# Start addresses of TensorE's operands in SBUF moved to multiples of 512 bytes

## The chip, the core and the metric

The kernel runs on one core of a Trainium2 chip. The metric is the device time of one execution in microseconds (us). A profile of one execution gives the start and the length of every instruction on TensorE (PE, and PEld for its weight loads), VectorE (DVE), ScalarE (ACT), GpSimd (POOL) and the queues that start transfers (SP and others).

## What is computed

One layer of a decoder trunk for 256 tokens of width 2048, in float32. Each of four branches (block attention, gated convolution, indexed sparse attention, attention into 256 memory tokens) reads columns of one wide projection of the normalized input:

```
xn = rms_norm(x, ln_g)
(a_q, a_k, a_v, a_g, c_b, c_c, c_h, c_g, s_q, s_k, s_v, s_g, m_q, m_g,
 i_q, i_k, i_w, r_a, r_c, r_s, r_m) = [xn @ w for w in cols]
...
y_c = c_b * short_conv(c_c * c_h, conv_w, conv_b) * jax.nn.silu(c_g)
...
merged = (sigmoid(r_a) * (y_a @ w_branch[0]) + sigmoid(r_c) * (y_c @ w_branch[1])
          + sigmoid(r_s) * (y_s @ w_branch[2]) + sigmoid(r_m) * (y_m @ w_branch[3]))
return x + merged @ w_out
```

A last RMSNorm follows. Nearly all work is matrix products of 256 rows with weights that are read once, 266 MB in all.

## The kernel before

Each float32 product is made of three products in float32r, a form that TensorE multiplies in one pass. `split` (L103) writes an operand as `hi`, the rounded value (a CAST on ScalarE, L104), and `lo`, the rest (a subtraction on VectorE, L105); then hi·hi, hi·lo and lo·hi are summed in PSUM. `split_weights` (L114) loads 1 MB of weights with a transfer on SP's queue into one of four `raw` buffers and splits it into pairs of `hi` and `lo`, four buffers each. The activations are split once and kept: `x_hl` (the normalized input), `m16a` and `m16b` (the memory tokens, `m_hl` in the code), `y` (a branch's gated result), `mt` (the merged result, in the place of `x_hl`), `x_sums`; in the attentions `part` and `pt`.

Two forms of product fill TensorE:

- `products_t` (L135, lines L138 to L140): the weights `hi` or `lo` are the stationary operand (128 columns), the activations the moving one (256 columns). The tile written is `acc` (or `first`). `project_t` makes all the sections that are wanted transposed.
- `products` (L157, lines L159 to L161): 128 columns of activations are stationary, 512 columns of `hi` or `lo` move. The tiles written are `w` (branch projections, activations `y`), `r` and `v` (gate and memory projections, activations `x_hl` or `m16a`/`m16b`), `o` (the last projection, activations `mt`; its last two blocks have 256 columns), and `m`, `z`, `r`, `x`, `y` in `by_halves` (L222), a form of the gate projections with fewer products and more additions. In the trace a product is written out<-moving,stationary.

Transposes (`pp`) take `ident` as the moving operand and float32 tiles (`pr`, `merged`) as the stationary one.

Tiles come from pools (L54 to L60). A pool's tiles lie one after another in each partition, from multiples of 32 bytes on, and the pools follow each other: `const`, `big`, `rawp`, `spl` (`hi`, `lo`), `prt` (`part`), `ptp` (`pt`), `tmp`. So the sum of the small constants sets where all large tiles begin, and the convolution's `u` ([128, 8, T + 2] float32, 8,256 bytes, in one place with `kt`) sets where everything behind it begins. All large tiles and all slices that TensorE reads are multiples of 512 bytes long, so within the large pools the remainder of the start by 512 is the same for all tiles of a group. In the built program before the change:

| tiles | first byte in the partition | remainder by 512 |
|---|---|---|
| `ident` | 16,768 | 384 |
| `x_col` / `m_col` | 18,944 / 20,000 | 0 / 32 |
| `x_hl`, `mt` | 24,352 | 288 |
| `qt`, `m16b`, `m16a`, `kt`, `x_sums`, `merged` | 57,120 and on | 288 |
| `vv`, `y` | 106,336 and on | 352 |
| `raw`, `hi`, `lo`, `part`, `pt` | 139,104 and on | 352 |
| `pr` | 220,064 | 416 |

The order of the instructions on each engine is set by a scheduler when the program is built. On POOL the first instructions are four loads of constants (`g_x`, `g_m`, `cw`, `cb`, L77 to L80), then `ident` and the masks. `g_x` is first read by `split_tokens` (L130).

## Time and profile before

| | |
|---|---|
| median of 3 runs | 1,399.23 us (1,397.75 to 1,400.73) |
| profiled execution | 1,398.06 us, its span 1,396.3 us |
| TensorE busy | 1,380.4 us (99%), 8,796 products |
| VectorE busy | 933.4 us (67%) |
| ScalarE busy | 729.2 us (52%) |
| POOL busy | 11.0 us (1%) |
| granted TensorE clock, mean | 0.997 |
| transfers | 269.5 MB, mean 193 GB/s |

TensorE's busy time is made of overlapping products whose ends are modelled: a product of 256 columns is listed with 276 to 281 ns, while the next one starts 113 to 118 ns after it. The pace is therefore read from starts, either in the timeline (first column: start in us) or as a window's length over the number of products in it.

### The profile page before, as it was taken

The page shows a single profiled execution, that of the slowest core. Times are in us where ns is not written, and L with a number is a line of the kernel's source. Part 1 is how long each engine was busy: PE and PEld are TensorE (multiplying, and loading weights), DVE is VectorE, ACT ScalarE, POOL GpSimd, SP SyncE. Part 2 cuts the span into 40 slices and gives each one's busy share as a digit, 9 for nine tenths or more (in the row PEclk, how much of TensorE's full clock was granted, in tenths as well). Part 3 has the DMA queues.
Part 4 walks back from the last instruction along what each step waited for, and adds up shares of the span by engine and source line. Part 5 has one row for each costly group of instructions (what it writes and reads, how often), then busy time and mean ns, then how long its engine had stood idle before and what let it go on. Part 6 is the DMA issues. An engine that isn't in the chain of part 4 may idle for free.

```text
span 1396.3 us, 21263 instructions
## 1 busy us (share of the span) xinstructions
PE 1380.4 (99%) x8796; PEld 1243.9 (89%) x8796; DVE 933.4 (67%) x1123; ACT 729.2 (52%) x991; POOL 11.0 (1%) x25
## 2 busy tenths in 40 slices
PE   9999999999999999999999999999999999999997
PEld 9998998789998898878999899878999998878887
DVE  7687764774848884596546885487547558787654
ACT  7663675453445684354445585445343345545443
POOL 1000000000000000000000000000000000000000
PEclk9999999999999999999999999999999999999999
DMA  9774545375554735537553746537555654736551
GB/s 343 291 271 173 191 156 180 128 266 189 172 197 133 254 128 183 189 135 247 188 193 133 243 150 211 182 125 266 183 181 187 225 192 148 265 130 241 183 197 73
DMA packets 49969, 269.49 MB, mean 193 GB/s; under 512 B 6656, under 2 KB 17456, under 8 KB 19024
## 3 DMA queue, kind: packets, MB, share of 16 engines
q1 hardware_dynamic: 48960, 264.03, 55.0%
q0 software_dynamic: 624, 3.31, 0.6%
q8 instruction: 69, 1.13, 0.3%
q10 hardware_dynamic: 288, 0.79, 0.1%
q14 instruction: 28, 0.23, 0.0%
HBM read 265.88 MB, written 2.10 MB: 192 GB/s over the span
## 4 chain that ended last, share of the span: by engine, by line
PE 85%; DVE 8%; DMA 3%; issue 2%; ACT 2%; SPq 0%; POOLq 0%; POOL 0%; DVEq 0%; ACTq 0%
PE acc L138 13%; PE acc L140 13%; PE acc L139 13%; DVE lo L105 5%; PE w L160 4%; PE w L161 4%; PE w L159 4%; PE r L159 4%; PE r L161 4%; PE r L160 4%; PE o L160 2%; PE o L161 2%; PE o L159 2%; DMA raw<-in_w_n 1%; PE y L160 1%
## 5 line engine op out<-in xcount | busy, mean ns | idle before, releaser
L105 DVE TENSOR_TENSOR lo<-raw,hi 128x1024 fp32r<-128x1024 f32 (+1 forms) x538 | 640.0, 1202 | 416.5 <-ACT hi L104 414.4
L104 ACT CAST hi<-raw 128x1024 fp32r<-128x1024 f32 (+1 forms) x538 | 552.2, 1032 | 547.8 <-PE acc L139 196.4
L139 PE MATMUL acc<-x_hl,hi 128*128 128x256 f32 x1520 | 426.0, 280 | 0.0
L138 PE MATMUL acc<-x_hl,hi 128*128 128x256 f32 x1520 | 425.4, 280 | 0.5 <-ACT qt L155 0.5
L140 PE MATMUL acc<-x_hl,lo 128*128 128x256 f32 x1520 | 425.8, 280 | 0.0
L140 PEld LDWEIGHTS acc<-x_hl,lo 128*128 128x128 f32 x1520 | 288.1, 190 | 0.1
L138 PEld LDWEIGHTS acc<-x_hl,hi 128*128 128x128 f32 x1520 | 284.8, 187 | 0.9 <-ACT qt L155 0.7
L139 PEld LDWEIGHTS acc<-x_hl,hi 128*128 128x128 f32 x1520 | 284.8, 187 | 0.2
L159 PE MATMUL w<-hi,y 128*128 128x512 f32 x256 | 99.9, 390 | 0.0
L161 PE MATMUL w<-hi,y 128*128 128x512 f32 x256 | 99.7, 389 | 0.0
L160 PE MATMUL w<-lo,y 128*128 128x512 f32 x256 | 99.6, 389 | 0.0
L159 PE MATMUL r<-hi,x_hl 128*128 128x512 f32 x248 | 98.3, 396 | 0.0
L161 PE MATMUL r<-hi,x_hl 128*128 128x512 f32 x248 | 97.9, 395 | 0.0
L160 PE MATMUL r<-lo,x_hl 128*128 128x512 f32 x248 | 97.6, 394 | 0.0
L159 PEld LDWEIGHTS w<-hi,y 128*128 128x128 f32 x256 | 48.1, 188 | 10.0
L161 PEld LDWEIGHTS w<-hi,y 128*128 128x128 f32 x256 | 48.1, 188 | 10.0
L160 PEld LDWEIGHTS w<-lo,y 128*128 128x128 f32 x256 | 48.1, 188 | 9.9
L161 PEld LDWEIGHTS r<-hi,x_hl 128*128 128x128 f32 x248 | 46.7, 188 | 10.6
L160 PEld LDWEIGHTS r<-lo,x_hl 128*128 128x128 f32 x248 | 46.7, 188 | 10.4
L159 PEld LDWEIGHTS r<-hi,x_hl 128*128 128x128 f32 x248 | 46.9, 189 | 10.2
L161 PE MATMUL o<-hi,mt 128*128 128x512 f32 (+1 forms) x160 | 55.3, 347 | 0.0
L160 PE MATMUL o<-lo,mt 128*128 128x512 f32 (+1 forms) x160 | 55.1, 346 | 0.0
(246 smaller groups left out, 1860.7 us busy)
## 6 DMA issues: line engine op xcount, KB each, us to landing
raw<-in_w_t SPq DMA_DIRECT2D x92, 1024.0 KB, 5.0
raw<-in_w_n SPq DMA_DIRECT2D x80, 1024.0 KB, 4.9
raw<-in_w_branch SPq DMA_DIRECT2D x32, 1024.0 KB, 5.3
raw<-in_w_out SPq DMA_DIRECT2D x16, 1024.0 KB, 4.8
raw<-in_w_mem_k SPq DMA_DIRECT2D x8, 1024.0 KB, 6.4
raw<-in_w_mem_v SPq DMA_DIRECT2D x8, 1024.0 KB, 5.5
raw<-in_w_t SPq DMA_DIRECT2D x16, 256.0 KB, 5.9
raw<-in_memT SPq DMA_DIRECT2D x2, 1024.0 KB, 8.8
```

Source lines behind the costliest of these rows:

```text
L104: nc.scalar.copy(out=hi, in_=src)
L105: nc.vector.tensor_sub(out=lo, in0=src, in1=hi.bitcast(F32))
L138: nc.tensor.matmul(o, lhsT=hi, rhs=a[:, 0], start=(k == 0), stop=False)
L139: nc.tensor.matmul(o, lhsT=hi, rhs=a[:, 1], start=False, stop=False)
L140: nc.tensor.matmul(o, lhsT=lo, rhs=a[:, 0], start=False, stop=(k == nk - 1))
L159: nc.tensor.matmul(o, lhsT=ah, rhs=hi, start=start, stop=False)
L160: nc.tensor.matmul(o, lhsT=ah, rhs=lo, start=False, stop=False)
L161: nc.tensor.matmul(o, lhsT=al, rhs=hi, start=False, stop=stop)
```

## The change

A tile `fill` of 56 float32 values (224 bytes) is added to the constants' pool and set to zero on POOL. The convolution's `u` gets a place of 8 · (T + 16) float32 values (8,704 bytes), of which it uses the first 8 · (T + 2) with the same row step as before.

```
     cb = const.tile([P, 8], F32, name="cb")
+
+    fill = const.tile([P, 56], F32, name="fill")
+    nc.gpsimd.memset(fill, 0.0)
     nc.gpsimd.dma_start(out=g_x, in_=ln_g)
...
     cc = to_heads("qt", C_C)
-    u = big.tile([P, 8, T + 2], F32, name="u", tag="kt")
+    u = big.tile([P, 8 * (T + 16)], F32, name="u", tag="kt")[:, :8 * (T + 2)].rearrange("p (c t) -> p c t", c=8)
     nc.gpsimd.memset(u[:, :, 0:2], 0.0)
```

With it the built program places the tiles so (the last byte used is 228,928, before 228,256):

| tiles | first byte in the partition | remainder by 512 |
|---|---|---|
| `ident` | 16,992 | 96 |
| `x_col` / `m_col` | 19,168 / 20,224 | 224 / 256 |
| `x_hl`, `mt` | 24,576 | 0 |
| `qt`, `m16b`, `m16a`, `kt`, `x_sums`, `merged` | 57,344 and on | 0 |
| `vv`, `y` | 107,008 and on | 0 |
| `raw`, `hi`, `lo`, `part`, `pt` | 139,776 and on | 0 |
| `pr` | 220,736 | 64 |

On TensorE, VectorE, ScalarE and SP the instructions stand in the same order as before, in the same shapes. On POOL one is added. At the start of the program POOL has, before the change (loads of `g_x`, `g_m`, `cw`, `cb`, then the first setups):

```order
6 L77 DMA g_x<-in_ln_g 128x16
7 L78 DMA g_m<-in_mem_ln_g 128x16
8 L79 DMA cw<-in_conv_w 128x24
9 L80 DMA cb<-in_conv_b 128x8
10 masks.py:197 MEMSET ident 128x128
```

And at the same place with the change:

```order
6 L79 MEMSET fill 128x56
7 L80 DMA g_x<-in_ln_g 128x16
8 L81 DMA g_m<-in_mem_ln_g 128x16
9 L82 DMA cw<-in_conv_w 128x24
10 L83 DMA cb<-in_conv_b 128x8
11 masks.py:197 MEMSET ident 128x128
```

The MEMSET of `fill` stands ahead of the four loads, and all that follows on POOL is one place later; line numbers behind it are three higher.

## Rows read from the trace of the kernel before

**Rows 1.** The page: engines' busy time; granted clock by fortieth; the chain by engine.
```profile
PE 1380.4 (99%) x8796; PEld 1243.9 (89%) x8796; DVE 933.4 (67%) x1123; ACT 729.2 (52%) x991; POOL 11.0 (1%) x25
...
PEclk9999999999999999999999999999999999999999
...
PE 85%; DVE 8%; DMA 3%; issue 2%; ACT 2%; SPq 0%; POOLq 0%; POOL 0%; DVEq 0%; ACTq 0%
```

**Rows 2.** Timeline of PE from 380 us: start us, length us, engine, line, operation.
```profile
380.07 0.28 PE L140 MATMUL acc<-x_hl,lo 128*128 128x256 f32 x1
...
384.94 0.28 PE L138 MATMUL acc<-x_hl,hi 128*128 128x256 f32 x1
```

**Rows 3.** Timeline of PE from 700 us.
```profile
700.12 0.28 PE L139 MATMUL acc<-x_hl,hi 128*128 128x256 f32 x1
...
704.95 0.28 PE L138 MATMUL acc<-x_hl,hi 128*128 128x256 f32 x1
```

**Rows 4.** Timeline of PE from 578 us.
```profile
578.07 0.39 PE L159 MATMUL w<-hi,y 128*128 128x512 f32 x1
...
582.83 0.39 PE L159 MATMUL w<-hi,y 128*128 128x512 f32 x1
```

**Rows 5.** Windows: by_halves, `r`, `o`; length, busy us by engine (count), clock, DMA share.
```profile
265.00:303.00 38.00, 37.15 (x161) 29.64 (x160) 32.93 (x31) 21.17 (x23) 0.00 (x0) 1.00 0.65 224
...
858.00:897.00 39.00, 39.00 (x169) 31.59 (x168) 17.77 (x15) 17.34 (x18) 0.00 (x0) 1.00 0.56 189
...
1307.00:1364.00 57.00, 57.00 (x251) 46.77 (x250) 31.45 (x31) 24.47 (x30) 0.00 (x0) 1.00 0.55 187
```

**Rows 6.** Transposes of `merged`: timeline of PE, and the line's lengths (min/median/max ns).
```profile
1227.41 1.04 PE L633 MATMUL pp<-ident,merged 128*128 128x128 f32 x8
...
L633 PE MATMUL pp<-ident,merged x32: 272/272/273, 1227.4 to 1306.9; 128*128 128x128 f32 x32
```

**Rows 7.** The start: timeline of POOL and ACT, and the landing of `g_x`.
```profile
1.24 0.70 POOL L77 DMA_DIRECT2D g_x<-in_ln_g  x1 [0.79 <-POOLq L706]
...
3.66 0.12 POOL L93 MEMSET mhalf<- 128x2 f32 x1
...
4.46 0.90 ACT L130 ACTIVATE x_hl<-xraw,g_x 128x256 fp32r<-128x256 f32 x2
...
DMA to landing us min/median/max: 2.9/2.9/2.9
```

**Rows 8.** Groups of weight loads by shape: count, busy us, mean ns.
```profile
L139 PEld LDWEIGHTS acc<-x_hl,hi 128*128 128x128 f32 x1504 | 282.6, 188 | 0.2
...
L633 PEld LDWEIGHTS pp<-ident,merged 128*128 128x128 f32 x32 | 3.7, 141 | 0.5
...
L285 PEld LDWEIGHTS pr<-ident,x_col 128*128 128x128 f32 x2 | 0.2, 134 | 0.0
```

**Rows 9.** Groups of products by shape: count, busy us, mean ns, idle before.
```profile
L139 PE MATMUL acc<-x_hl,hi 128*128 128x256 f32 x1504 | 421.5, 280 | 0.0
...
L159 PE MATMUL w<-hi,y 128*128 128x512 f32 x256 | 99.9, 390 | 0.0
...
L160 PE MATMUL m<-lo,x_sums 128*128 128x512 f32 x84 | 34.1, 406 | 3.3 <-DVE lo L105 3.3
```

**Rows 10.** Windows, instructions of tile `acc` alone: length, PE busy us (count), PEld.
```profile
357.00:433.00 76.00, 76.00 (x671) 75.85 (x670) 0.00 (x0) 5.49 (x15) 1.00 0.53 181
...
665.00:756.00 91.00, 90.62 (x768) 90.60 (x768) 0.00 (x0) 5.72 (x15) 1.00 0.53 182
...
986.00:1168.00 182.00, 180.95 (x1536) 181.05 (x1536) 6.22 (x16) 5.60 (x15) 1.00 0.56 190
```

**Rows 11.** Timeline of PE from 156.3 us, in the memory attention.
```profile
156.39 0.28 PE L140 MATMUL acc<-x_hl,lo 128*128 128x256 f32 x1
156.50 0.28 PE L354 MATMUL yp<-pt,part 128*128 128x256 f32 x1
...
157.69 0.28 PE L355 MATMUL yp<-pt,part 128*128 128x256 f32 x1
```

## The prediction

> **What bounds the kernel now.** [...] Busy TensorE says nothing of its pace, because matmuls overlap, so the timeline comes next: the distance from one start to the next.

> [...] From 380.07 to 384.94 us there are 43 steps of 256 columns, 113.3 ns each [rows 2]. From 700.12 to 704.95 us there are 41 steps of the same form on the same tiles, 117.8 ns each [rows 3]. From 578.07 to 582.83 us there are 21 steps of 512 columns, 226.7 ns each [rows 4]. The window from 858 us, with one product reaching over its edge, gives (39.0 + 0.4) us / 169 = 233 ns, and the window from 1307 us 57.4 / 251 = 229 ns [rows 5].

> [...] Where moving and stationary operand begin at the same remainder of 512 bytes (`w`: `hi` and `y`, both 352), 512 columns stay at 226.7; where they don't (`r`, `o`: 352 against 288), they lie at 229 to 233 [rows 4, 5].

> **The change part by part.** No instruction changes its place or its shape; what is new is one MEMSET on POOL and other start addresses. Every float32r operand (`x_hl`, `mt`, `m16a`, `m16b`, `y`, `hi`, `lo`, `part`, `pt`) goes from 288 or 352 to 0 past a multiple of 512.

> *The MEMSET* stands ahead of the four constants' loads on POOL. Its neighbours in kind are 0.10 to 0.12 us long; `g_x` is loaded from 1.24 us and lands 2.9 us later, at 4.14, while its first reader, behind a CAST on ScalarE, starts at 4.46 [rows 7]. So 0.3 us are hidden; without that cover the cost would be 0.1 us. I take nothing.

> *The padded `u`* keeps its row step of T + 2; only what lies behind it moves. Nothing.

> *VectorE, ScalarE and DMA addresses* move as well. No row shows the same operation at another remainder, so I take nothing, and bound it by VectorE's 8% of the chain.

> *Transposes.* `ident` moves from 384 to 96 and `pr` from 416 to 64, so these are not at multiples of 512. There are about 100 of them; 7 ns either way is 0.7 us. Nothing.

> *The streams* are the term that counts. No row shows a float32r operand that starts at a multiple of 64 bytes: 288 and 352 are both 32 past one. [...]
> [...]
> [...]

> [...]

> The counts: the groups by shape hold 5,520 products of 256 columns (the three largest groups have 1,504 each) and 3,084 of 512 (of them three groups of 256 for `w`) [rows 9]. By stretch, the 256-column products at 113.3 are 576 + 671 of `acc` and some 385 of the first and the last stage, together 1,632; those at 117.8 are 768 + 1,536 = 2,304 [rows 10]; the other 1,584 lie in the attention stretches, which switch between the levels, and I price them midway at 115.6. The sum over the floor:
> - 256 columns: 1,632 x 3.6 + 2,304 x 8.1 + 1,584 x 5.9 ns = 5.9 + 18.7 + 9.3 = 33.9 us.
> - 512 columns: `w` 768 x 10.4 = 8.0 us; the other 2,316 at about 229.5, so 13.2 each = 30.6 us.
> - Together 72.5 us.

> Not all of it reaches the end. In the first by_halves VectorE is busy for 32.9 of 38 us and TensorE, for 37.2, already has pauses [rows 5]; `m` waits for `lo` [rows 9]. Transfers are at 0.65 of their engines there, so 5% more demand is no new bound. I take the chain for this: TensorE holds 0.85 x 1,396 = 1,187 us of it, while the products fill 5,520 x 116 + 3,084 x 229 ns = 1,347 us, so 88% of the gain counts: 64 us. The profiled execution took 1,398.06 us (span 1,396.3 and 1.8 around it); less 64 is 1,334. It lay 1.2 us under the median, so 1,335 against the runs shown.

> [...]

> **The rivals.**
> [...]

> *Only the pairing counts.* All operands then share a remainder, as `y` and `hi` do now, and all streams run at the lowest level known, 113.3 and 226.7. That saves 2,304 x 4.5 + 1,584 x 2.3 + 2,316 x 2.8 ns = 20.5 us, 88% of it 18: 1,381. [...]

> *Slower: equal remainders collide.* In the attention, `part` and `pt` share the remainder 352, and eleven products of 256 columns in a row from 156.50 to 157.69 us lie 1.19 / 10 = 119 ns apart, where neighbouring `acc` products take 113 [rows 11]. If equal remainders cost this in every 256-column stream, the rise is 1,632 x 5.7 + 2,304 x 1.2 + 1,392 x 3.4 = 16.8 us, less the 6.5 us that 512 columns win: 10, 88% of it 9, so 1,408. With 512 columns at 233 as well it would be about 1,426. It decides against the change from a 256-column step of 117.0 ns on (6.5 us over 5,328 products above the present mean of 115.8). Against it: that run is short, and `w` with equal remainders is the calmest stream there is.

> **How the numbers follow.** The surcharge goes: 0.42, 1,335 (1,312 to 1,353). Only the pairing: 0.18, 1,381. Nothing: 0.14, 1,399. Slower: 0.26, 1,408 to 1,426. The range 1,315 to 1,408 holds nearly all of the first, the second, the third and half of the last, some 0.82. A measurement of this kernel tells 0.2% from no change: faster 0.60, same 0.14, slower 0.26.

> **What would show it.** Right: steps of 109 to 110 ns where [rows 2, 3] stand and 216 where [rows 4] stand, 134 in place of 141 for the weight load of `merged`, one level and not two. If the steps are 113.3 and 226.7 throughout, it was the pairing; if [rows 2] and [rows 3] come back as they are, nothing. Wrong in size: TensorE waiting longer in by_halves, with VectorE above 90% there. Wrong altogether: 256-column steps of 118 ns or more in most stretches.

## The result: 1.1% slower, and where it lies

The changed kernel takes 1,414.29 us (median of 4 runs, 1,413.15 to 1,414.42) against 1,399.22 us before (4 runs, 1,397.75 to 1,400.73). The ratio is 1.0106, with a 95% interval of 1.0088 to 1.0123: slower, where I had forecast 1,335 us.

The page of the changed kernel, the rows that answer to [rows 1] (busy time by engine, granted clock by fortieth, the chain by engine):

```profile
PE 1396.2 (99%) x8796; PEld 1263.7 (89%) x8796; DVE 933.8 (66%) x1123; ACT 729.2 (52%) x991; POOL 11.2 (1%) x26
...
PEclk9999999999999999999999999999999999999999
...
PE 87%; DVE 7%; DMA 2%; issue 2%; ACT 2%; SPq 0%; POOLq 0%; POOL 0%; DVEq 0%; ACTq 0%
```

Everything that was added lies on TensorE: 15.8 us more busy time with the same 8,796 products, at the same granted clock, 0.997 of full speed in both profiles. VectorE and ScalarE are busy as long as before within 0.4 us, and TensorE's share of the chain has grown from 85% to 87%.

The timeline shows the step from one start to the next. The stretch near 380 us, which answers to [rows 2], first and 38th row (start us, length us, engine, line, operation; line numbers are three higher than before):

```profile
379.76 0.28 PE L143 MATMUL acc<-x_hl,lo 128*128 128x256 f32 x1
...
384.20 0.28 PE L141 MATMUL acc<-x_hl,hi 128*128 128x256 f32 x1
```

The stretch from 704.76 us, which answers to [rows 3], first and 44th row:

```profile
704.76 0.28 PE L142 MATMUL acc<-x_hl,hi 128*128 128x256 f32 x1
...
709.92 0.28 PE L143 MATMUL acc<-x_hl,lo 128*128 128x256 f32 x1
```

4.44 / 37 and 5.16 / 43 are both 120.0 ns, where 113.3 and 117.8 stood. The two levels have become one, and it is slower than either. The windows of `acc` alone say the same for whole streams (length, busy us of PE and count, PEld, DVE, ACT, clock, DMA share, GB/s; answer to [rows 10]). The last product's listed length reaches 0.16 us over its step, so (92.31 - 0.16) / 768 = 120.0 ns:

```profile
363.00:444.00 81.00, 80.77 (x672) 80.56 (x671) 0.00 (x0) 5.67 (x15) 1.00 0.50 170
675.00:768.00 93.00, 92.31 (x768) 92.29 (x768) 0.00 (x0) 5.79 (x15) 1.00 0.52 178
999.00:1185.00 186.00, 184.47 (x1536) 184.45 (x1536) 6.25 (x16) 5.83 (x16) 1.00 0.54 186
```

Products of 512 columns went the other way. Timeline of `w` and of `r`, first and 28th row of each (answer to [rows 4, 5]):

```profile
587.82 0.39 PE L162 MATMUL w<-hi,y 128*128 128x512 f32 x1
...
593.94 0.39 PE L162 MATMUL w<-hi,y 128*128 128x512 f32 x1
```

```profile
869.68 0.39 PE L162 MATMUL r<-hi,x_hl 128*128 128x512 f32 x1
...
875.80 0.39 PE L162 MATMUL r<-hi,x_hl 128*128 128x512 f32 x1
```

Both give 6.12 / 27 = 226.7 ns. `w` stayed where it was, and `r` came down from 233. But 233 was not its only level before: at the same remainders it went at 229 ns near 217 us. First and 18th row of each, before the change:

```profile
217.09 0.39 PE L160 MATMUL r<-lo,x_hl 128*128 128x512 f32 x1
...
220.98 0.39 PE L159 MATMUL r<-hi,x_hl 128*128 128x512 f32 x1
```

```profile
854.80 0.40 PE L159 MATMUL r<-hi,x_hl 128*128 128x512 f32 x1
...
858.77 0.40 PE L161 MATMUL r<-hi,x_hl 128*128 128x512 f32 x1
```

3.89 / 17 = 229 and 3.97 / 17 = 233 ns; the prediction priced all of these at about 229.5.

Summed over all consecutive starts in the two traces (steps of 109 to 126 ns for 256 columns, of 222 to 240 ns for 512, which leaves pauses out): 256 columns rise from 633.9 us (5,463 steps, mean 116.0) to 655.7 us (5,469 steps, 119.9); 512 columns fall from 692.1 us (3,021 steps, 229.1) to 685.2 us (3,017 steps, 227.1). That is +21.7 - 6.9 = +14.8 us (with the means on equal counts, 3.85 x 5,466 and 1.98 x 3,019 ns, +21.0 - 6.0 = +15.0). The medians differ by 15.1 us and the two profiled executions by 16.4 us, so nearly all of the loss is explained by these two lines.

### The profile page after: what moved, and what is told of

It is laid out like the page before. It is cut to its first block, busy times and chain, and to the rows that moved or that the text cites. A ratio compares the mean times of both kernels' runs of the same rounds, so it can differ in the third digit from the quotient of the medians.

```text
span 1412.6 us, 21263 instructions
## 1 busy us (share of the span) xinstructions
PE 1396.2 (99%) x8796; PEld 1263.7 (89%) x8796; DVE 933.8 (66%) x1123; ACT 729.2 (52%) x991; POOL 11.2 (1%) x26
## 4 chain that ended last, share of the span: by engine, by line
PE 87%; DVE 7%; DMA 2%; issue 2%; ACT 2%; SPq 0%; POOLq 0%; POOL 0%; DVEq 0%; ACTq 0%
PE acc L141 14%; PE acc L143 14%; PE acc L142 14%; DVE lo L108 4%; PE w L163 4%; PE w L164 4%; PE w L162 4%; PE r L162 3%; PE r L163 3%; PE r L164 3%; PE o L162 2%; PE o L163 2%; PE o L164 2%; DMA raw<-in_w_n 1%; PE y L163 1%
## 5 line engine op out<-in xcount | busy, mean ns | idle before, releaser
L142 PE MATMUL acc<-x_hl,hi 128*128 128x256 f32 x1520 | 431.2, 284 | 0.0
L143 PE MATMUL acc<-x_hl,lo 128*128 128x256 f32 x1520 | 431.0, 284 | 0.0
L141 PE MATMUL acc<-x_hl,hi 128*128 128x256 f32 x1520 | 430.5, 283 | 0.0
L142 PEld LDWEIGHTS acc<-x_hl,hi 128*128 128x128 f32 x1520 | 290.8, 191 | 0.2
L141 PEld LDWEIGHTS acc<-x_hl,hi 128*128 128x128 f32 x1520 | 290.7, 191 | 0.2
L162 PE MATMUL o<-hi,mt 128*128 128x512 f32 (+1 forms) x160 | 55.4, 347 | 0.0
L164 PE MATMUL o<-hi,mt 128*128 128x512 f32 (+1 forms) x160 | 55.3, 347 | 0.0
```

The costliest lines, as they stand in the source:

```text
L141: nc.tensor.matmul(o, lhsT=hi, rhs=a[:, 0], start=(k == 0), stop=False)
L142: nc.tensor.matmul(o, lhsT=hi, rhs=a[:, 1], start=False, stop=False)
L143: nc.tensor.matmul(o, lhsT=lo, rhs=a[:, 0], start=False, stop=(k == nk - 1))
L162: nc.tensor.matmul(o, lhsT=ah, rhs=hi, start=start, stop=False)
L164: nc.tensor.matmul(o, lhsT=al, rhs=hi, start=False, stop=stop)
```

## The experiments

In what follows the *distance* is where the stationary operand starts in a partition, less where the moving one starts, modulo 512 bytes. Before the change it was 64 for `acc` (352 less 288) and 448 for `r` and `o` (the other way round); after it, 0 everywhere.

| run | distance, 256 / 512 columns | mean step, 256 / 512 columns | median us | ratio to before (95%) |
|---|---|---|---|---|
| before | 64 / 448 | 116.0 / 229.1 | 1,399.2 | |
| after | 0 / 0 | 119.9 / 227.1 | 1,414.3 | 1.0106 (1.0088 to 1.0123) |
| e1, filling alone | 64 / 448 | 116.4 / 229.1 | 1,399.6 | 1.0001 (0.999 to 1.0011) |
| e2, padded `u` alone | 0 / 0 | 119.9 / 227.1 | 1,414.1 | 1.0104 (1.0089 to 1.0119) |
| e3, `u` T + 14 | 448 / 64 | 117.5 / 231.7 | 1,410.8 | 1.0080 (1.0065 to 1.0095) |
| e4, `u` T + 8 | 256 / 256 | 119.9 / 227.1 | 1,414.1 | 1.0105 (1.0090 to 1.0120) |
| v1, two views | 64 / 0 | 116.5 / 227.1 | 1,396.5 | 0.9986 (0.9975 to 0.9996) |
| b2, before with seven products more | 64 / 448 | 114.2 / 229.1 | 1,389.9 | 0.9933 (0.9918 to 0.9948) |
| v2, two views and the seven | 64 / 0 | 114.4 / 227.1 | 1,384.2 | 0.9896 (0.9881 to 0.9911) |
| a2, after with the seven | 0 / 0 | 119.9 / 227.1 | 1,414.1 | 1.0107 (1.0088 to 1.0125) |

Distances are those of the long streams; the means are over all steps, as above. `w` has its own pair of operands, with distance 0 in every kernel here.

### e1 and e2: one half of the change each

e1 keeps the filling, e2 the padding:

```
+    fill = const.tile([P, 56], F32, name="fill")
+    nc.gpsimd.memset(fill, 0.0)
```

```
-    u = big.tile([P, 8, T + 2], F32, name="u", tag="kt")
+    u = big.tile([P, 8 * (T + 16)], F32, name="u", tag="kt")[:, :8 * (T + 2)].rearrange("p (c t) -> p c t", c=8)
```

> Of the change only the filling stands, u is T + 2 wide as before. The x operands (x_hl, mt, m16) start at a remainder of 0 modulo 512 bytes as after the change, the pieces of the weights (hi, lo) and y at 64, so that the distance between the two operands of a product is the 64 bytes that it was before (288 and 352). Theory P (the distance between the two starts decides): products of 256 columns step by 113.3 or 117.8 ns as before, those of 512 columns by 226.7 or 229 to 233 ns, about 1399 us. Theory S (the start of the streamed operand decides, here 0 as after the change): 120.0 and 226.7 ns as after the change, about 1414 us.

> Of the change only the padding of u stands, without the filling. All operands start at a remainder of 288 modulo 512 bytes: no start is at a multiple of 64, as before the change, but the distance is 0, as after it. Theory P (the distance decides): 120.0 ns for 256 columns and 226.7 ns for 512 columns, about 1414 us. Theory S (the start decides): the levels of before, 113.3 or 117.8 and 226.7 to 233 ns, about 1399 us.

The windows of `acc` in e1, in the places of [rows 10]:

```profile
358.00:434.00 76.00, 76.00 (x671) 76.00 (x671) 0.00 (x0) 5.24 (x14) 1.00 0.54 181
666.00:757.00 91.00, 90.35 (x768) 90.54 (x768) 0.00 (x0) 5.45 (x15) 1.00 0.53 182
```

And in e2:

```profile
362.00:443.00 81.00, 80.69 (x672) 80.49 (x672) 0.00 (x0) 5.28 (x14) 1.00 0.51 170
675.00:768.00 93.00, 92.32 (x768) 92.29 (x768) 0.00 (x0) 5.79 (x15) 1.00 0.52 178
```

e1 puts the x operands at a multiple of 512 and has the steps and the time of before (76.00 / 671 = 113 and 90.35 / 768 = 118 ns). e2 has not one operand at a multiple of 64, and has the 120.0 ns and the time of after. So the start itself has no price at the remainders tried (e2, with all of them at 288, and after, with all at 0, take 1,414.1 and 1,414.3 us): the changed kernel loses all of its time by the padding of `u`, which takes away the 64 bytes between the two operands of a product. Theory S falls, P holds.

### e3 and e4: other distances

The same line with T + 14 and with T + 8 in place of T + 16, and the filling.

> With the filling, u T + 14 wide: x operands at 0, the pieces and y at 448, so that the second operand starts 64 bytes below the first modulo 512 and not 64 above it as before. Theory P with a distance that counts in both directions alike: the levels of before, about 1399 us. Theory P with a direction: in the kernel before, the stream o had its moving operand at 352 and its stationary one at 288, and its 256-column products all stepped by 113.3 ns, while merged's with 288 and 352 went by 113.3 or 117.8; the swap then gives merged's products 113.3 ns throughout, about 1385 us, and o's 512-column products something else than 229 ns. Theory S (the start of the streamed operand, 0): about 1414 us.

> With the filling, u T + 8 wide: x operands at 0, the pieces and y at 256, as far from each other modulo 512 bytes as two starts can be. Theory P, where nearness makes the two reads collide: 113.3 and 226.7 ns throughout; from the sums over the steps of the trace before (14.8 us above 113.3 in the products of 256 columns, 7.4 us above 226.7 in those of 512) about 1377 us, less what is not on the path. Theory P with a period of 256 bytes: 120.0 ns and 226.7 ns, 1414 us. Theory S (start 0): 1414 us as well, so that this run tells P with nearness from the others and e1 and e2 tell P from S.

The windows of `acc` in e3 at the two places, and its `r` (timeline, first and 23rd row):

```profile
362.00:442.00 80.00, 79.50 (x672) 79.29 (x672) 0.00 (x0) 5.66 (x15) 1.00 0.51 172
675.00:767.00 92.00, 90.62 (x768) 90.56 (x768) 0.00 (x0) 6.08 (x16) 1.00 0.53 179
```

```profile
867.80 0.39 PE L161 MATMUL r<-hi,x_hl 128*128 128x512 f32 x1
...
872.93 0.39 PE L162 MATMUL r<-lo,x_hl 128*128 128x512 f32 x1
```

In e3 `acc` steps by 118 ns in both places, (79.50 - 0.16) / 672 and (90.62 - 0.16) / 768, and `r` by 5.13 / 22 = 233 ns. The distance counts with its sign, but not as I had it: 448 did not give `acc` the 113.3 ns that `o` has there, and 1,410.8 us is none of the three times that I had named. e4, as far apart as two starts can be, repeats distance 0 to the nanosecond. Nearness is not the point; the pattern seems to repeat every 256 bytes. s1 measured that directly.

### s1: the cost by itself, at 32 distances

```
+    for d in range(0, 512, 16):
+        burst(f"s{d:03d}x", T, steps256(0, d))
+    for d in range(0, 512, 16):
+        burst(f"m{d:03d}x", T, steps256((512 - d) % 512, 0))
+    for d in range(0, 512, 16):
+        burst(f"w{d:03d}x", NB, steps512(0, (512 - d) % 512))
```

In `s` the stationary operand is shifted, in `m` and `w` the moving one.

> The disputed cost by itself: all of the kernel's work is left out. Three tiles are filled once, then TensorE alone runs bursts of float32r products while the other engines and the queues are all but idle. For each distance d from 0 to 496 bytes in steps of 16 (where the stationary operand starts, less where the moving one starts, modulo 512) there are three bursts: s, 48 products of 256 columns with the stationary operand shifted; m, the same with the moving operand shifted instead; w, 24 products of 512 columns with the moving operand shifted. Three bursts l (48 products) alternate stationary operands at distance 0 (two of three) and at 64, 128 or 192. Theory P (the distance decides, by the two reads of TensorE alone): at d = 0 and 256 steps of 120.0 ns in s and m and 226.7 ns in w, at 64 steps of 113.3 or 117.8 ns in s and m, at 448 117.8 ns, w at 64 233 ns and at 448 229 ns; s and m agree at each d. [...]

Windows of single bursts (`m000x`, `m064x`, `m192x`, `m256x`, `w000x`, `w064x`; length, busy us of PE and count, PEld, ACT, clock, DMA share, GB/s):

```profile
203.00:209.00 6.00, 5.85 (x48) 5.83 (x48) 0.00 (x0) 1.00 0.00 0
...
225.00:232.00 7.00, 5.63 (x48) 5.55 (x48) 0.35 (x1) 1.00 0.01 2
...
271.00:277.00 6.00, 5.81 (x48) 5.73 (x48) 0.00 (x0) 1.00 0.01 3
...
293.00:300.00 7.00, 5.92 (x48) 5.83 (x48) 0.27 (x1) 1.00 0.00 0
...
384.00:390.00 6.00, 5.63 (x24) 4.43 (x24) 0.00 (x0) 1.00 0.00 0
...
406.00:413.00 7.00, 5.76 (x24) 4.51 (x24) 0.57 (x1) 1.00 0.00 0
```

The steps of the bursts, from the same trace without the first six of each, in ns (the first burst, `s000x`, contains the start and is left out):

| distance | s | m | w |
|---|---|---|---|
| 0 | | 120.0 | 226.6 |
| 64 | 113.3 | 113.3 | 233.2 |
| 128 | 118.7 | 119.9 | 232.8 |
| 144 | 120.0 | 114.0 | 230.7 |
| 192 | 113.3 | 117.8 | 228.9 |
| 256 | 120.0 | 120.0 | 226.6 |
| 320 | 113.3 | 113.3 | 233.2 |
| 384 | 118.7 | 120.0 | 232.8 |
| 448 | 113.3 | 117.8 | 228.9 |

The other multiples of 16 lie between 116.6 and 123.5 ns and between 231 and 235 ns (400 repeats 144). Three things follow.

- With transfers at a share of 0.00 to 0.01 and only one copy per burst on ScalarE, all levels of the kernel are there: 113.3, 117.8, 120.0, 226.7, 229 and 233. If contention with what VectorE, ScalarE and the transfers read and write made the upper levels, one step would have stood at all distances. That falls: TensorE makes them by itself, with addresses alone changed.
- A distance and the one 256 further on agree within 0.2 ns in every row of the table, and in all but one of the others (s at 48 and 304 differ by 5.7). The period is 256 bytes.
- For 256 columns, 0 is among the worst distances and 64 the best; for 512 columns, 0 is the best. The change moved both widths to 0, where one loses and the other wins.

I had expected s and m to agree at each distance. At 192 they don't (113.3 and 117.8), nor at 144 (120.0 and 114.0), and both differences come back 256 bytes further on. Which operand is shifted doesn't decide it at 448: e3 shifted the stationary one, as s does, and its `acc` went at 117.8, as m does. The same distance can settle at either, so it takes something besides the distance. For the distances that are no multiples of 64 no run separates the two. The three bursts l, whose distances alternate, went at 117.8 to 118.9 ns.

### s2: what sets the level at one distance

> All of the kernel's work is left out; bursts of products alone, as in s1. In the traces with distance 64 a stream of 256 columns that follows 512-column products without a pause stays at 117.8 ns to its end (665 to 756 us, 987 to 1168 us of the kernel before), while nearly every one that starts behind a wait stays at 113.3. Bursts k: 23 to 25 products of 512 columns (distance 64 above, then 0), then one thing between, then 72 products of 256 columns at distance 64. Between stand: nothing; one float32 product of 128 columns; a short wait for VectorE; one float32r product of 16, 64, 128, 192 columns at distance 64; one of 256 columns at distance 0 or 128. Theory L (the two reads lock in a phase that the start sets): the streams with nothing between go at 117.8 ns throughout, and some of the things between turn them to 113.3 throughout. Theory H (the level depends on what else the kernel runs at the time): all of them go alike. Bursts c: 48 products with the high stationary pieces at 64 or 192 and the low pieces and the second moving operand at 0, 64, 128 or 192 each; if a combination leaves more room between the reads than 113.3 ns shows, it would lie below; I expect none below 113.3.

```
+                run(o, NB, steps512(c, 23 + r))
+                nc.scalar.copy(out=keep, in_=o)
+                between(kind, name)
+                o = bank(name + "a", "a")
+                run(o, T, steps256(64, 64, 0, 72))
```

Windows of four bursts of 72 products (columns as in s1). The first two follow 512 columns at distance 0, with nothing between (`k000a`) and with a product of 64 columns between (`k040a`); the other two follow 512 columns at distance 448, with 16 columns between (`k130a`) and with 192 (`k160a`):

```profile
402.00:412.00 10.00, 8.64 (x72) 8.62 (x72) 0.37 (x1) 1.00 0.00 0
...
569.00:578.00 9.00, 8.42 (x72) 8.24 (x72) 0.00 (x0) 1.00 0.00 0
...
150.00:160.00 10.00, 8.73 (x72) 8.54 (x72) 0.24 (x1) 1.00 0.00 0
...
278.00:287.00 9.00, 8.37 (x72) 8.25 (x72) 0.17 (x1) 1.00 0.00 0
```

Each row but the first contains a first step of 140 to 201 ns behind the short product; what follows it is steady after some six steps.

The scheduler did not leave everything between where the program had put it: the product behind the wait ran after the 29th product of the stream in all six bursts, and in two bursts (`k110a`, `k111a`) the float32 product ran tens of microseconds earlier. These eight streams began with nothing between. Windows of `k102a` and `k110a`, then the start of `k110a` (timeline):

```profile
53.00:62.50 9.50, 8.64 (x72) 8.62 (x72) 0.12 (x1) 1.00 0.00 0
...
67.00:76.00 9.00, 8.35 (x72) 8.34 (x72) 0.15 (x1) 1.00 0.01 2
```

```profile
67.18 0.39 PE L71 MATMUL k110w<-lo,xs 128*128 128x512 f32 x1
67.41 0.40 PE L71 MATMUL k110a<-xs,hi 128*128 128x256 f32 x2
```

8.64 and 8.35 us, less the 0.16 that the last product reaches over, are 117.8 and 113.8 ns a step, the first six included. By the steps in the trace:

- With distance 0 ahead and nothing between, the streams go at 117.8 from the first step on (six of six; three of them up to the product in their middle).
- With distance 0 ahead, one product of 16, 64, 128 or 192 columns at distance 64, one of 256 columns at distance 0 or 128, and one of float32 turned all of them to 113.3 within some six steps (21 of 21).
- With distance 448 ahead, nothing between does not settle it: `k102a` stayed at 117.8, five others went to 113.3 within some six steps. 16, 64 and 128 columns left them at 117.8 (9 of 9); 192 columns (3 of 3), the one float32 product that did stand between and 256 columns (5 of 6) ended at 113.3. So the effect of 192 columns can't be told from that of nothing here.
- The six bursts with a wait pause at the product in their middle, and end at 117.8; three of them had gone at 113.3 before it. The two bursts that contain the start of the program have pauses of 10 and 22 us and end at 113.3. A wait by itself, then, chooses neither setting.
- The bursts of 512 columns themselves have two settings at 448: 8 of 26 go at 233.3 ns and 18 at 229 (one more contains the start). At distance 0 all 27 go at 226.7.

Theory H falls, since these bursts run alone and differ. Theory L holds this far: at distance 64 the stream has two steady settings (called phases below; no run looks inside), and one is kept until something breaks the stream. Behind 512 columns at distance 0, as `w` is in the kernel, what stands directly between chooses it; behind distance 448 it is open what does. The same may hold for the 229 and 233 of `r`; no run asked. Of the 32 combinations of pieces none went below 113.2.

This bears on the 113.3 and 117.8 that the prediction saw on the same addresses: in the traces of before, e1 and v1 alike, the streams near 665 and 987 us, which follow `w` directly, stand at 117.8 to their end. The one near 357 us stands at 113.3. It does not start behind a wait, as I had it before s2, but directly behind float32 products (`lg`), which is one of the things that turned a stream in s2; no run takes them out (before, timeline):

```profile
356.27 0.60 PE L456 MATMUL lg<-it 128*128 128x256 f32 x2
356.52 0.47 PE L138 MATMUL acc<-x_hl,hi 128*128 128x256 f32 x1
```

### v1: each width at its own distance

```
-    def parts_tiles(w=NB, c=NB):
-        return [spl.tile([P, 2 * NB], F32R, name=n, tag=n).rearrange("p (k c) -> p k c", c=w)[:, :, :c]
-                for n in ("hi", "lo")]
+    def parts_tiles(w=NB, c=NB, up=0):
+        return [spl.tile([P, 2 * NB + 64], F32R, name=n, tag=n)[:, up:up + 2 * NB]
+                .rearrange("p (k c) -> p k c", c=w)[:, :, :c] for n in ("hi", "lo")]
...
-                hi, lo = parts_tiles(w, c)
+                hi, lo = parts_tiles(w, c, 16 if w == TB else 0)
```

> A version made from P: all operands at 288 as in e2 (u padded, no filling), but each piece of the weights has 256 bytes more room, and the products of 256 columns use it from 64 bytes further on (distance 64), those of 512 columns from its start (distance 0). Room for it comes from two masks that share their places with two rows no longer needed; no instruction moves. P: 256 columns at 113.3 or 117.8 ns as before, 512 columns at 226.7 ns; the 6.9 us that the 512-column steps lost in the trace after the change are won, 88% of it 6 us: 1393 us. If a distance has to hold for all products alike to count, 1399 or 1414 us.

512 columns come to 227.1 ns as expected (2.0 ns on 3,012 steps, 6.0 us). But 256 columns rose by 0.4 ns on 5,466 steps, 2.2 us: `o` and parts of the attention settled at 117.8 this time. 1,396.5 us is 0.14% faster, where I had expected 0.4%. The distances do hold for each width by itself; what the first setting gives is not in hand yet.

### b2, v2 and a2: the phase, in the kernel itself

```
+    def shift_phase(o, lhsT, rhs):
+        if fresh["phase"]:
+            nc.tensor.matmul(o, lhsT=lhsT, rhs=rhs, start=True, stop=True)
+        fresh["phase"] = False
...
+            if k == 0:
+                shift_phase(spare[:min(P, c)], hi[:, 0:min(P, c)], act(0)[:, 0, :192])
```

> The kernel before with its addresses (distance 64), and seven products of 192 columns more: one ahead of each stream of 256 columns that follows products of 512, written to columns of the accumulator's bank that nobody reads. A few products in the attention change places with their neighbours. In s2 a product of 192 columns turned the stream after it to 113.3 ns in three of three with the 512-column products at distance 64. Theory L (the start of a stream sets its phase): the streams that stood at 117.8 ns (176 products near 325 us, 768 near 665 us, 1,536 near 987 us) go to 113.3 ns; 2,480 x 4.5 = 11.1 us, 88% of it 9.8, less seven products of about 0.1 us: 1390 us. Theory H (the level comes from what else the kernel runs in these stretches): 1399 to 1400 us with the levels where they were.

> v1 (256 columns at distance 64, 512 columns at distance 0) with the same seven products of 192 columns. Theory L: all long streams of 256 columns at 113.3 ns, 512 columns at 226.7; the streams at 117.8 ns in v1 (176, 768, 1,536 and 191 products) are 2,671 x 4.5 = 12.0 us, 88% of it 10.6: 1396.5 - 10.6 + 0.7 = 1387 us. Theory H: 1397 us.

> The kernel after the change with its addresses (distance 0 everywhere) and the same seven products of 192 columns as in b2 and v2. Theory L with P: the phase has two settings at distance 64 alone; at distance 0 all streams of 256 columns stay at 120.0 ns however they start, about 1414 to 1415 us. If the lost time were a matter of how the streams start, and not of the distance, the 2,480 products behind the seven would go to 113.3 ns: 2,480 x 6.7 = 16.6 us, 88% of it 14.6, about 1400 us.

The beginning of the stream near 664 us in b2 (timeline): the product of 192 columns, and the steps behind it.

```profile
664.28 0.39 PE L171 MATMUL w<-hi,y 128*128 128x512 f32 x1
664.50 0.25 PE L139 MATMUL acc<-x_hl,hi 128*128 128x192 f32 x1
664.59 0.30 PE L145 MATMUL acc<-x_hl,hi 128*128 128x256 f32 x1
```

Windows of `acc` in b2, then in v2, then in a2, for the second and third stream of [rows 10] (the product of 192 columns is counted with them):

```profile
664.00:753.00 89.00, 87.33 (x769) 87.32 (x769) 0.00 (x0) 5.98 (x16) 1.00 0.55 186
982.00:1158.00 176.00, 174.38 (x1537) 174.36 (x1537) 6.12 (x16) 5.74 (x15) 1.00 0.58 196
```

```profile
662.00:751.00 89.00, 87.34 (x769) 87.32 (x769) 0.00 (x0) 5.95 (x16) 1.00 0.55 186
979.00:1155.00 176.00, 174.38 (x1537) 174.36 (x1537) 6.11 (x16) 6.00 (x16) 1.00 0.57 196
```

```profile
675.00:769.00 94.00, 92.23 (x769) 92.02 (x768) 0.00 (x0) 6.19 (x16) 1.00 0.51 173
999.00:1186.00 187.00, 184.58 (x1537) 184.41 (x1537) 6.25 (x16) 6.19 (x16) 1.00 0.54 184
```

(174.38 - 0.16) / 1,537 = 113.4 ns in b2 and v2, where before had 117.8. Seven products took 8.5 us off the kernel before, at unchanged addresses (1,398.4 and 1,389.9 us in that comparison; theory L had 1,390). In a2 the same seven do nothing, (184.58 - 0.16) / 1,537 = 120.0: no run shows a faster setting at distance 0. v2 is the fastest kernel here, 1,384.2 us, faster than before by 14.2 us and than after by about 30 (medians of two comparisons). Not all streams gained: the last 191 products of `o` and some 54 of `acc` near 139 us stood at 113.3 before and at 117.8 in b2 and v2, 1.1 us together; no run asks why.

## Why the prediction was wrong, point by point

- **TensorE's steps set the time: right.** The whole difference lies in them, and VectorE never became the bound. The window of by_halves that answers to [rows 5], 5.9 us later in the program:

```profile
270.90:308.90 38.00, 37.15 (x162) 29.61 (x161) 32.99 (x31) 21.08 (x23) 0.00 (x0) 1.00 0.65 224
```

- **MEMSET, padded row, VectorE, ScalarE, transfers, transposes at nothing: right.** e1, which has the MEMSET, takes as long as before; POOL is busy 0.2 us more, VectorE 0.4 us, ScalarE as long as in [rows 1]; transposes have their 272 ns [rows 6].
- **The streams, priced over a floor of 109.7 and 216.3 ns: this step failed.** No run shows that floor, or what the 1,312 to 1,353 us around the forecast were worked out from: the lowest levels that the runs show are 113.2 ns for 256 columns (s2) and 226.6 for 512 (s1). The term that was to save 72.5 us cost 14.8 instead: aligned operands have 120.0 ns for 256 columns and still 226.7 for 512, and e1 and e2 show that the start has no price, 0 and 288 alike. The gain from aligned starts was my estimate, and no row showed an aligned operand. The weight load of `merged` doesn't show one either: now that `merged` is aligned it takes 140 ns, not the 134 that I had named ([rows 8] before, this row after; count, busy us, mean ns).

```profile
L636 PEld LDWEIGHTS pp<-ident,merged 128*128 128x128 f32 x32 | 3.7, 140 | 0.5
```

- **The upper levels come from the pairing of the two starts: half right.** For 512 columns it was: 229.1 to 227.1 ns, 6.9 us against the rival's 2,316 x 2.8 = 6.5. For 256 columns equal remainders are the slow end. And 256 columns have two levels at one distance, which the prediction saw in [rows 2, 3] but left unexplained; s2 and b2 show them to be settings that a stream keeps. The 229 to 233 of 512 columns was one such pair too, in `r`, and the prediction took it for a spread.
- **The rival that equal remainders collide: this is what happened, at a price that stood in the rows.** Eleven products of `part` and `pt` in [rows 11] showed 119 ns at distance 0; after the change the same eleven and the `acc` products on both sides of them step by 120.0 ns (1.20 / 10 in the two rows below). I gave it 0.26 because the run is short and because `w`, with equal remainders, was the calmest stream. But `w` has 512 columns, and the row of the right width was the burst.

```profile
161.32 0.28 PE L357 MATMUL yp<-pt,part 128*128 128x256 f32 x1
...
162.52 0.28 PE L358 MATMUL yp<-pt,part 128*128 128x256 f32 x1
```

- **88% of it on the path: too small.** The rival's sum was 10 us and its time 1,408; with 120.0 ns throughout the sum is 14.8 us, and all of it reached the end. So did v2's gain: 9.2 and 5.8 us in the steps of 256 and 512 columns, less 0.7 for the seven products, against 14.2 in the time. The time fell inside that rival's 1,408 to 1,426, of which the range held only half.
- **That the pairing of the two starts has a price: right.** At equal lengths and an equal clock (1.00 in the windows of s1), the distance alone moves a step of 256 columns between 113.3 and 120.0 ns. The weight loads show it from the other side: those of `acc` take 192 ns after the change and 188 before [rows 8].

```profile
L142 PEld LDWEIGHTS acc<-x_hl,hi 128*128 128x128 f32 x1504 | 288.6, 192 | 0.2
```

What stays open: why the period is 256 bytes, why 512 columns prefer distance 0 and 256 columns 64, and what chooses the setting at distance 448. No distance in steps of 16 bytes gave less than 113.3 and 226.6 ns (s1).

## What to carry to other kernels

A round start address was neither a cost nor a gain in itself here (1,414.1 us with all starts at 288, 1,414.3 with all at 0); what counted for the streams of float32r products was how far apart the moving and the stationary operand start, modulo 256 bytes, and it differed by width (113.3 to 123.5 ns for 256 columns, 226.6 to 235 for 512, in s1). So change one operand's address against the other's, measure the step of each width separately, and where both widths occur don't move all operands to one remainder. Where a long stream shows two levels on the same addresses, look at what comes directly before it: one short product ahead of each of seven streams gave 0.7% here (b2), and with the distances sorted by width 1.0% (v2).
